# Decays at the chunk ends of an RWKV-7 layer: through DRAM rows in place of two TensorE transposes

## Chip, cores and metric

The kernel runs on one core of one Trainium2 chip. The metric is the device time of one execution in microseconds (us), as the median of several runs. Engines are called as in the profile: PE (TensorE, matrix products and transposes), DVE (VectorE), ACT (ScalarE), POOL (GpSimd) and SP (SyncE, whose queue issues nearly all DMAs here).

## The reference, cut to what matters

The model is a trunk of two layers over 256 tokens of width 1024. Each layer has a half-step SwiGLU FFN, a mixer, and another half-step FFN; the mixer of layer 0 is a short convolution, that of layer 1 is RWKV-7 time mixing with 16 heads of 64 channels. Only the recurrence of the time mixing is touched:

```python
w_log = -softplus(-(w0 + tanh(xw @ w1) @ w2)) - 0.5
decay = exp(-exp(w_log))                       # per token and channel
def step(S, inp):                              # S: one 64x64 state per head
    r_t, w_t, k_t, v_t, a_t, b_t = inp
    sa = einsum('bhij,bhj->bhi', S, a_t)
    S = S * w_t[:, :, None, :] + sa[..., None] * b_t[:, :, None, :] + v_t[..., None] * k_t[:, :, None, :]
    y = einsum('bhij,bhj->bhi', S, r_t)
    return S, y
```

Tokens are worked in chunks of 64. From one chunk to the next the state of each head is multiplied, channel by channel, by the product of the 64 decays of the chunk. These products are what the change fetches in another way.

## The kernel before, in words

Everything but the recurrence is dense products: FFN in layer 0, convolution, FFN, FFN of layer 1, the inputs of the time mixing, then the stage of the heads (some 700 to 885 us of the span), then the last FFN. Every fp32 product is made of three matmuls on a high and a low part (`product`, L110 to L114).

In the stage of the heads (`rwkv_heads`, L829) the work is cut into 8 units n: four groups q of four heads, each with two halves t of 128 tokens, and each unit holds two chunks of 64 tokens. Four generators give the steps of a unit:

- `front(n)` (L841): gates and decays of the unit. A product with a lower triangle (`cum`) sums the logs of the decays; ACT makes from it `P` (L874), the running product of the decays with tokens on the partitions, then `PP` (L875) and later `iP` (L883). POOL makes `rt` from `P` (L877), DVE finishes `PP` (L881); PE transposes `PP`, `rt`, `b`, `iP` (tile `wT`), and multiplies them into the matrices `G`. DVE masks these into `br` (L930) and `ar` (L933). Eight small DMAs copy `b` and `iP` from partition to partition into `bkt`. In its last step, PE transposes `P` (tile `PT`, two transposes of 128x128), and ACT copies from the result four columns, the chunk ends, into `pc` (L940 to L944).
- `wkv_inverse` (L490), run through `inverse(n)` (L949): the inverse of a triangular matrix by doubling, products `pair` on PE, `pb` on DVE, `xr` on ACT. At its steps 6 and 8 it issues the loads `hvu` for the unit's two chunks.
- `chain(n)` (L960, `wkv_chunk` L542): the recurrence over the chunks: `rc` on ACT (L558), products `ch` on PE, and at the end of a chunk DVE multiplies the new state by `pc` (L581).
- `finish(n)` (L967): norm and gate of the output.

Between these, `filler()` puts pieces of dense products into PE's stream (tile `pj`), whose weights come as loads `hl_n` of 512 KB from DRAM into 8 buffers, issued by `feed()` on SP.

The order of all of this is written by hand. `score` (L1069) is a list of strings in which F, I, C, N, `*` and L mean the next step of the front of the unit after next, of the next unit's inverse, of the chain, of the finish, a filler, and a feed. PE's and SP's instructions keep the order of the program (`mm`, `tp` and `load` ask for it, L48 to L57), and ACT's and DVE's do so inside `manual_schedule`. So every engine is a queue: an instruction that waits holds all behind it.

Two sizes matter for the change. `P` has one buffer: `T2` (L835) makes a tile with `bufs=1`, so the front of the next unit writes its `P` into the memory that the unit before has used. And the PSUM banks that `front` uses (`tr_bank`, L87) are two in turn: one front takes `z`, `cum`, `wT`, `wT`, `G0`, `G1` and `PT`, seven in all, each of which waits until the bank before the last is read out.

Further, SP's DMAs signal on eight semaphores in turn (they are called DMAHW0 to DMAHW7 in lists of waits), and a DMA is issued when the eighth before it has landed.

Of the kernel before, what the change touches and what calls it, by code (L numbers as in the profile page):

```python
# [10 lines left out]
F32 = mybir.dt.float32  # L11
# [14 lines left out]
class Trunk:  # L26
# [802 lines left out]
    def rwkv_heads(self, pool, prm, krv, lora, gT, g2, rows, row_tile, P, loaded, follow,  # L829
                   first_weights, first):  # L830
        nc = self.nc
# [4 lines left out]
        s4 = lambda name, b=2: pool.tile([128, 4], F32, name=name, bufs=b)  # L836
        us, o = [], {}
# [3 lines left out]
        def front(n):  # L841

            q, t = divmod(n, 2)
            ts, cs = slice(t * 128, t * 128 + 128), slice(q * 256, q * 256 + 256)
            u = dict(bon=s4("bon", 4), hvu=[])
            us.append(u)
            k, r = (krv[q, i][:, t] for i in "kr")
            P, PP, kk, am, rt = (T2(i) for i in ("P", "PP", "kk", "am", "rt"))
# [10 lines left out]
            s, a = sa[:, 0], sa[:, 1]  # L859
# [5 lines left out]
            cp = self.tr_bank("cum")  # L865
# [47 lines left out]
            f = lambda z: z.rearrange("p c q t -> p (c q) t")  # L913
# [11 lines left out]
            yield  # L925
            nc.vector.copy_predicated(x0, by4(self.strict).bitcast(mybir.dt.uint32), f(gb[:, :, :, 0]))
            u["inv"] = inverse(n)
            next(u["inv"])
            yield
# [7 lines left out]
                    self.load(bkt[ro, c, :, e], self.tokens(iP, c, e))  # L937
                yield

            cp = self.tr_bank("PT")[:, 0:256]  # L940
            for p in range(2):
                self.tp(cp[:, p * 128:p * 128 + 128], P[:, p * 128:p * 128 + 128])
            u["pc"] = s4("pc", 3).rearrange("p (q c) -> p q c", q=2)
            nc.scalar.copy(u["pc"], cp.rearrange("p (q c s) -> p q c s", q=2, c=2)[:, :, :, 63])  # L944
            nc.vector.tensor_reduce(u["bon"], hd(am), AX.X, ALU.add)
            nc.vector.tensor_scalar(u["bon"], u["bon"], 0.5, None, op0=ALU.mult)
            yield
# [1 line left out]
        def inverse(n):  # L949
            q, t = divmod(n, 2)  # L950
            for i, _ in enumerate(self.wkv_inverse(pool, us[n], n % 2, self.pair[:, :, 0:256])):
                if i in (6, 8):
                    c = i // 2 - 3
                    h = pool.tile([128, 2, 2, 64], F32, name="hvu", bufs=6)
                    for e in range(2):
                        self.load(h[64 - 64 * e:128 - 64 * e, :, e], self.tokens(krv[q, "v"][:, t], c, e))
                    us[n]["hvu"].append(h)
                yield
# [93 lines left out]
        def filler():  # L1052
# [27 lines left out]
            'CNCL*NCC*NL*CC*LNNCNC*LCC*NNL*CC*L',  # L1080
        )
        fronts = (step for n in range(8) for step in front(n))
        feed()
        for _ in score[0]:
# [118 lines left out]
```

## Time and profile before

| what | value |
|---|---|
| runs before | 1086.74, 1086.78, 1088.98 us; median 1086.78 |
| profiled execution | 1088.63 us, its span 1086.9 us |
| PE busy | 1060.1 us, 98% of the span |
| DVE, ACT, POOL busy | 686.5, 528.8, 100.1 us (63%, 49%, 9%) |
| DMA | 259.39 MB, 239 GB/s on average, q1 busy 72.3% of 16 engines |
| chain that ended last | PE 73%, issue 18%, DVE 5% |

The span runs from the first to the last instruction; some 1.7 us of the execution's time lie around it. The chain that ended last is followed back from the last instruction, at each step to what released it. "Issue" in it is time in which an engine waited for nothing that the profile shows. The table is an average over stages; what a change in the stage of the heads is worth must be read there.

### The profile page before, as it was taken

What the parts mean: (1) busy time and instruction counts of PE and PEld (TensorE: products, weight loads), DVE (VectorE), ACT (ScalarE), POOL (GpSimd) and SP (SyncE); (2) the same over time, 40 slices, a digit from 0 to 9 for tenths busy, and PEclk for the clock granted to TensorE, in tenths of its full rate; (3) what the DMA queues carried; (4) which work ended last, traced back from release to release, by engine and by line L of the source; (5) the groups of instructions that cost most, each with busy time, mean ns of one, the idle gap of its engine ahead of it and who ended that gap; (6) DMA issues with size and microseconds to landing.
All of it is one profiled execution on the core that took longest, in us unless ns stands there. A gap on an engine that the chain in (4) does not pass through costs nothing.

```text
span 1086.9 us, 16688 instructions
## 1 busy us (share of the span) xinstructions
PE 1060.1 (98%) x6480; PEld 872.9 (80%) x6480; DVE 686.5 (63%) x980; ACT 528.8 (49%) x781; POOL 100.1 (9%) x179
## 2 busy tenths in 40 slices
PE   7999999999999999999999999999998999999997
PEld 5888888788878888887888888998877668888885
DVE  5665554787667565466665544758998866555444
ACT  7555543655555554455555442344645426444342
POOL 7000000000130000000000001122423210000000
PEclk9999999999999999999999999999999999999999
DMA  9999867698779996778988871866555855656541
GB/s 287 298 292 289 297 224 247 210 360 271 236 266 339 302 307 233 246 242 280 332 295 271 320 271 51 312 233 192 170 145 148 252 172 183 187 184 213 184 164 39
DMA packets 178167, 259.39 MB, mean 239 GB/s; under 512 B 24238, under 2 KB 142758, under 8 KB 178088
## 3 DMA queue, kind: packets, MB, share of 16 engines
q1 hardware_dynamic: 178088, 258.32, 72.3%
q8 instruction: 51, 0.84, 0.3%
q14 instruction: 28, 0.23, 0.1%
HBM read 216.34 MB, written 38.80 MB: 235 GB/s over the span
## 4 chain that ended last, share of the span: by engine, by line
PE 73%; issue 18%; DVE 5%; ACT 1%; DMA 1%; SPq 1%; POOL 0%; POOLq 0%; DVEq 0%; ACTq 0%
PE gu L113 10%; PE gu L114 10%; PE gu L112 10%; PE acc L113 5%; PE acc L114 5%; PE acc L112 5%; PE pj L112 2%; PE pair L114 2%; PE pair L113 2%; PE pair L112 2%; PE ci L113 2%; PE ci L114 2%; PE ci L112 2%; PE pj L113 2%; PE pj L114 2%
## 5 line engine op out<-in xcount | busy, mean ns | idle before, releaser
L107 DVE TENSOR_TENSOR lo_gu<-raw_gu,hi_gu 128x2048 fp32r<-128x2048 f32 (+2 forms) x92 | 198.4, 2160 | 110.2 <-ACT hi_gu L106 108.0
L113 PE MATMUL gu<-lo_gu,xh 128*128 128x512 f32 x640 | 253.5, 396 | 2.8 <-DVE lo_gu L107 2.7
L114 PE MATMUL gu<-hi_gu,xl 128*128 128x512 f32 x640 | 253.3, 396 | 0.0
L112 PE MATMUL gu<-hi_gu,xh 128*128 128x512 f32 x640 | 251.1, 395 | 0.7 <-ACT xh L178 0.7
L106 ACT CAST hi_gu<-raw_gu 128x2048 fp32r<-128x2048 f32 (+2 forms) x92 | 164.9, 1796 | 34.9 <-DMA raw_gu<-in_ffn_w_gu_dram 12.0
L107 DVE TENSOR_TENSOR lo_o<-raw_o,hi_o 128x2048 fp32r<-128x2048 f32 x48 | 109.2, 2291 | 110.5 <-ACT hi_o L106 109.2
L113 PEld LDWEIGHTS gu<-lo_gu,xh 128*128 128x128 f32 x640 | 120.9, 189 | 28.0 <-DVE lo_gu L107 4.3
L106 ACT CAST hi_o<-raw_o 128x2048 fp32r<-128x2048 f32 x48 | 90.7, 1908 | 103.4 <-PE acc L114 61.5
L112 PEld LDWEIGHTS gu<-hi_gu,xh 128*128 128x128 f32 x640 | 120.9, 189 | 25.0 <-ACT xh L178 1.1
L114 PEld LDWEIGHTS gu<-hi_gu,xl 128*128 128x128 f32 x640 | 120.8, 189 | 23.6 <-DVE xl L180 0.4
L113 PE MATMUL acc<-lo_o,ah 128*128 128x512 f32 (+1 forms) x316 | 122.4, 387 | 1.4 <-DVE lo_o L107 1.4
L114 PE MATMUL acc<-hi_o,al 128*128 128x512 f32 (+1 forms) x316 | 122.5, 388 | 0.0
L112 PE MATMUL acc<-hi_o,ah 128*128 128x512 f32 (+1 forms) x316 | 117.5, 388 | 0.0
L150 POOL TENSOR_TENSOR rs<-ms,fixed 128x1 f32<-128x1 f32 x14 | 11.2, 798 | 819.7 <-DVE ms L148 819.5
L345 ACT ACTIVATE s<-gu,rs 128x256 f32<-128x256 f32 x80 | 38.0, 475 | 98.4 <-PE gu L114 98.3
L113 PEld LDWEIGHTS acc<-lo_o,ah 128*128 128x128 f32 x316 | 59.4, 188 | 13.6 <-DVE lo_o L107 1.8
L112 PEld LDWEIGHTS acc<-hi_o,ah 128*128 128x128 f32 x316 | 59.4, 188 | 11.9
L114 PEld LDWEIGHTS acc<-hi_o,al 128*128 128x128 f32 x316 | 59.4, 188 | 11.9
L117 ACT CAST ah<-aT 128x512 fp32r<-128x512 f32 x44 | 25.8, 585 | 82.5 <-PE aT L351 82.5
L349 DVE SCALAR_TENSOR_TENSOR a<-gu,rs,s 128x256 f32<-128x256 f32 x80 | 38.3, 480 | 36.4 <-ACT s L345 36.4
L601 ACT CAST hl_p<-hl_p 128x512 fp32r<-128x512 f32 x72 | 44.3, 624 | 29.5 <-DMA hl_p<-in_rwkv_w_rkv_dram 16.9
L602 DVE TENSOR_TENSOR hl_p<-hl_p 128x512 fp32r<-128x512 f32 x72 | 48.2, 686 | 8.0 <-ACT hl_p L601 8.0
(270 smaller groups left out, 1662.8 us busy)
## 6 DMA issues: line engine op xcount, KB each, us to landing
raw_gu<-in_ffn_w_gu_dram SPq DMA_DIRECT2D x164, 512.0 KB, 5.6
raw_o<-in_ffn_w_d_dram SPq DMA_DIRECT2D x44, 1024.0 KB, 5.9
parts<-hl_p SPq DMA_DIRECT2D x72, 512.0 KB, 7.0
hl_n<-parts SPq DMA_DIRECT2D x52, 512.0 KB, 4.7
hl_p<-in_rwkv_w_rkv_dram SPq DMA_DIRECT2D x48, 256.0 KB, 7.4
raw_ci<-in_conv_w_in_dram SPq DMA_DIRECT2D x14, 512.0 KB, 6.9
raw_ci<-in_conv_w_in_dram SPq DMA_DIRECT2D x4, 1024.0 KB, 10.0
raw_o<-in_conv_w_out_dram SPq DMA_DIRECT2D x4, 1024.0 KB, 8.7
```

Source lines behind the costliest of these rows:

```text
L106: nc.scalar.copy(hi[:, ks], raw[:, ks])
L107: nc.vector.tensor_tensor(lo[:, ks], raw[:, ks], hi[:, ks].bitcast(F32), ALU.subtract)
L112: keep(mm(out, xh, wh, start=start, stop=False))
L113: keep(mm(out, xh, wl, start=False, stop=False))
L114: keep(mm(out, xl, wh, start=False, stop=stop))
L117: keep(self.nc.scalar.copy(hi, src))
L150: self.last_rs = nc.gpsimd.tensor_tensor(rs, ms[:, 1:2], self.nhalf[:, 0:1], ALU.pow)
L345: act = nc.scalar.activation(s, ps[t][:, 0:256], AF.Silu, scale=rstd[t])
L349: nc.vector.scalar_tensor_tensor(a, ps[t][:, 256:512], rstd[t], s, ALU.mult, ALU.mult)
L601: nc.scalar.copy(hi, lo)
L602: nc.vector.tensor_tensor(lo.bitcast(F32R), lo, hi.bitcast(F32), ALU.subtract)
```

## The change

`P` is no longer transposed. At the end of the front, two DMAs of one row each (partitions 63 and 127 of `P`, 256 channels, 1 KB) store the two chunk ends into a new DRAM tile `ends`. At step 4 of the unit's inverse, two DMAs read these rows back, so that each partition gets its channels: 256 pieces of 4 bytes each. The consumer of `pc` (L581) stays.

```diff
-            cp = self.tr_bank("PT")[:, 0:256]
-            for p in range(2):
-                self.tp(cp[:, p * 128:p * 128 + 128], P[:, p * 128:p * 128 + 128])
-            u["pc"] = s4("pc", 3).rearrange("p (q c) -> p q c", q=2)
-            nc.scalar.copy(u["pc"], cp.rearrange("p (q c s) -> p q c s", q=2, c=2)[:, :, :, 63])
+            u["ends"] = self.dram.tile([2, 256], F32, name=f"ends{n}")
+            for c in range(2):
+                self.load(u["ends"][c:c + 1], P[64 * c + 63:64 * c + 64])
             nc.vector.tensor_reduce(u["bon"], hd(am), AX.X, ALU.add)
...
             for i, _ in enumerate(self.wkv_inverse(pool, us[n], n % 2, self.pair[:, :, 0:256])):
+                if i == 4:
+                    us[n]["pc"] = pc = s4("pc", 3).rearrange("p (c q) -> p q c", q=2)
+                    with nc.allow_non_contiguous_dma("a channel on each partition"):
+                        for c in range(2):
+                            self.load(pc[:, :, c], us[n]["ends"][c].rearrange("(q p) -> p q", p=128))
                 if i in (6, 8):
```

On PE the eight pairs of transposes go, and nothing else of the stage moves. At the end of front 0 (`z` is the first product of front 1):

```order
 L113 MATMUL pj<-hl_n,xvh 128x256
 L114 MATMUL pj<-hl_n,xvl 128x256
-L57 MATMUL PT<-fixed,P 128x128 x2
 L54 MATMUL z<-w_5291,wT 128x256
 L54 MATMUL z<-a_5293,aT 128x256
```

The two transposes are gone, and with them one turn of the two PSUM banks: `z` now takes the bank of `G0`, where it took that of `G1`.

On SP, at the end of front 1 (it follows the eight `bkt` DMAs of the unit; `parts` are the split weights in DRAM):

```order
 L50 DMA hl_n<-parts_2825 128x1024
 L50 DMA hl_n<-parts_2912 128x1024
+L50 DMA ends_6176<-P 1x256 x2
 L50 DMA hl_n<-parts_2914 128x1024
+L50 DMA pc<-ends_6176 128x2x1 x2
 L50 DMA hvu<-pv 64x2x64 x2
 L50 DMA hl_n<-parts_3001 128x1024
```

The stores stand behind two weight loads, and the loads of `pc` one weight load later, ahead of `hvu`. At the end of front 0 it is two weight loads, the stores, three weight loads, `pc`. In fronts 2 to 6 the stores come straight behind `bkt`; in front 7 they stand behind two weight loads and four loads for the last FFN, with `pc` straight behind them.

On ACT, in front 2, with what each instruction waits for (semaphores of engines, and of DMAs as DMAHW), before:

```order
-L508 COPY xr_6250<-pair 128x512 [waits DVE_49]
-L874 ACTIVATE P<-cum,fixed 128x256 [waits DVE_49]
-L875 ACTIVATE PP<-PP,fixed 128x256
-L558 COPY rc<-ch 128x128 [waits PE_49]
-L508 COPY xr_6291<-pair 128x512 [waits DVE_49,Activation_49]
```

And with the change:

```order
+L508 COPY xr_6249<-pair 128x512 [waits DVE_49]
+L874 ACTIVATE P<-cum,fixed 128x256 [waits DMAHW4_49,DMAHW3_49,DVE_49]
+L875 ACTIVATE PP<-PP,fixed 128x256
+L558 COPY rc<-ch 128x128 [waits PE_49]
+L508 COPY xr_6290<-pair 128x512 [waits DVE_49,Activation_49]
```

`P` of a front now also waits for two DMAs, the stores of the front before, which read its buffer. All fronts from 1 to 7 have this wait. `PP`, `rc` and the next `xr` stand behind it on ACT.

## Rows read from the trace of the kernel before

**Rows 1.** Busy time of the engines in two stretches (columns in the header).
```profile
core 0: us, PE busy (x) PEld busy (x) DVE busy (x) ACT busy (x) POOL busy (x), PEclk, DMA share, GB/s
720.00:760.00 40.00, 39.18 (x543) 33.66 (x543) 27.88 (x71) 18.94 (x50) 8.61 (x13) 1.00 0.68 217
...
800.00:840.00 40.00, 36.31 (x550) 29.29 (x548) 35.66 (x93) 20.75 (x59) 13.79 (x18) 1.00 0.56 150
```

**Rows 2.** Tile PT: duration ns min/median/max, first and last start.
```profile
L57 PE MATMUL PT<-fixed,P x16: 271/272/299, 721.3 to 856.0; 128*128 128x128 f32 x16
L944 ACT COPY pc<-PT x8: 162/162/168, 721.7 to 856.3; 128x4 f32<-128x4 f32 x8
```

**Rows 3.** PE timeline at some removed transposes: start us, us, and idle before.
```profile
755.07 0.41 PE L57 MATMUL PT<-fixed,P 128*128 128x128 f32 x2 [0.36 <-DVE br L930]
...
755.41 0.46 PE L54 MATMUL pair<-xr,p 64*64 64x64 f32 x16
...
794.22 0.31 PEld L574 LDWEIGHTS ch<-hvu,bkt 128*64 128x64 f32 x8 [0.16 <-ACT y L570]
...
832.90 0.41 PE L57 MATMUL PT<-fixed,P 128*128 128x128 f32 x2 [1.30 <-DVE br L930]
```

**Rows 4.** Waits of PE, 640 to 900 us: total us, times, longest.
```profile
PE PT L57 <- DVE br L930: 1.9, 3, 1.3
...
PE z L54 <- DVE ar L933: 0.6, 2, 0.4
```

**Rows 5.** SP's timeline: third weight load after front 0, and after front 1.
```profile
725.44 0.38 SPq L50 DMA_DIRECT2D hl_n<-parts  x1
...
744.25 0.38 SPq L50 DMA_DIRECT2D hl_n<-parts  x1
```

**Rows 6.** DMAs issued at 724.97, 729.55, 729.96 and 743.77 us: KB, us to landing.
```profile
hl_n<-parts SPq DMA_DIRECT2D x1, 512.0 KB, 4.2
...
hl_n<-parts SPq DMA_DIRECT2D x1, 512.0 KB, 6.4
...
hvu<-pv SPq DMA_DIRECT2D x1, 32.0 KB, 6.2
...
hl_n<-parts SPq DMA_DIRECT2D x1, 512.0 KB, 4.9
```

**Rows 7.** DMA issued at 723.63 us, behind no weight load: KB, us to landing.
```profile
bkt<-iP SPq DMA_DIRECT2D x1, 32.0 KB, 1.9
```

**Rows 8.** ACT timeline: P of fronts 1 and 2, and rc behind the latter.
```profile
727.08 0.47 ACT L874 ACTIVATE P<-cum,fixed 128x256 f32<-128x256 f32 x1 [0.27 <-DVE PP L873]
...
742.93 0.47 ACT L874 ACTIVATE P<-cum,fixed 128x256 f32<-128x256 f32 x1
...
743.70 0.25 ACT L558 COPY rc<-ch 128x128 f32<-128x128 f32 x1
```

**Rows 9.** DVE and PE timelines behind P of front 1.
```profile
727.98 0.66 DVE L881 SCALAR_TENSOR_TENSOR PP<-kk,PP 128x256 f32<-128x256 f32 x1 [0.21 <-ACT PP L875]
...
729.36 0.38 PE L57 MATMUL wT<-fixed,PP 128*128 128x128 f32 x2
```

**Rows 10.** PE timeline behind P and rc of front 2.
```profile
744.25 0.40 PE L54 MATMUL ch<-rc,tt 64*64 64x64 f32 x8
```

**Rows 11.** SP's hvu at the place of front 7's stores, and its landing.
```profile
860.21 0.62 SPq L50 DMA_DIRECT2D hvu<-pv  x1
...
hvu<-pv SPq DMA_DIRECT2D x1, 32.0 KB, 6.7
```

**Rows 12.** Last bkt of fronts 2 and 6 (SP), P of fronts 3 and 7 (ACT).
```profile
755.14 0.61 SPq L50 DMA_DIRECT2D bkt<-iP  x1
...
761.10 0.48 ACT L874 ACTIVATE P<-cum,fixed 128x256 f32<-128x256 f32 x1
...
830.19 0.61 SPq L50 DMA_DIRECT2D bkt<-iP  x1
...
839.50 0.48 ACT L874 ACTIVATE P<-cum,fixed 128x256 f32<-128x256 f32 x1
```

## Prediction

> **What bounds the kernel now.** I read four views: busy time by stretch, the tile and the waits of the removed work, the timelines of SP, ACT and PE around the new wait, and the landing times of single DMAs.
>
> In the stage of the heads PE is busy 39.2 of 40 us while fronts 1 to 3 run (720 to 760 us) and still 36.3 of 40 at 800 to 840, where DVE has 35.7 [rows 1]. The clock is granted in full in both stretches. So time taken from PE is worth nearly its whole length early in the stage and less later on; and since PE's queue is in order, a wait of PE in this stage is time lost to the end: what follows is dense products again, which no earlier engine can shorten.
>
> **What goes.** Sixteen transposes of 272 ns and eight ACT copies of 162 ns [rows 2]. ACT is half idle; its 1.3 us count nothing by themselves. For PE the pair takes less than twice 272 ns, since the two overlap: the product after it starts 0.34 us behind it (755.07 to 755.41) [rows 3]. Eight pairs: 2.7 us. With them go the waits of the PSUM turn: PT waited for `br` 1.9 us in three places, and `z` for `ar` 0.6 us in two [rows 4]; `z` will wait for `br`, which DVE makes earlier. The upper bound of the gain is thus 2.7 + 1.9 + 0.6 = 5.2 us, the lower bound nothing.
>
> I don't take the whole. Fronts 0 and 1 give nothing, because PE runs into the new wait right behind them (below). Front 2 gives 0.5 (the pair, and part of its 0.36 us wait). Fronts 3 and 5 give some 0.6 each with the wait of `z`. In front 4 the product two places on stood waiting for an ACT copy anyway (`y`, 0.16 us) [rows 3], so nothing comes through. In front 6 PT waited 1.30 us [rows 3], but the same copies stand behind it; I take 0.5. Front 7 gives 0.3. That is 2.5 us; as DVE is as busy as PE from front 4 on [rows 1], I take **2.0 us**.
>
> **What comes: a wait of ACT for a store.** `P` has one buffer. The next front's `P` could be written as soon as POOL and PE had read the old one; now it must wait until two rows have been stored to DRAM, and the store stands on SP behind whatever SP issues before it. So the price is: landing of the stores minus the time at which `P` wants to start, less the slack until PE needs what hangs on it.
>
> Front 0 to 1. The stores come where SP issues its third weight load, at 725.44 us [rows 5]. Ahead of them are two loads of 512 KB; the second, issued at 724.97, takes 4.2 us and lands at 729.2 [rows 6]. How does a small DMA behind a big one land? The row for it: a load issued at 729.55 takes 6.4 us (735.95), and `hvu`, 32 KB, issued 0.4 us behind it, takes 6.2 (736.16) [rows 6]: 0.2 us after the big one. A small DMA with nothing big ahead of it takes 1.9 [rows 7]. Between these ends I take the first, since two big loads do stand ahead: the stores land at 729.4. `P` of front 1 started at 727.08 [rows 8], so it is 2.3 us late. On it hang `PP`, DVE's product (done at 728.64) and PE's transposes of `PP` at 729.36 [rows 9]: slack 0.7. **PE stalls 1.6 us.**
>
> Front 1 to 2. The stores come at the place of the load issued at 744.25 [rows 5], behind one issued at 743.77 that takes 4.9 us: 748.7 [rows 6]. SP itself is late here, as the load of `pc` of unit 0 held it until 729.4 plus two issues, which I price at 0.6 each like `hvu` [rows 11]: 730.6, against the 729.55 of the load that followed. Of this 1.1 us some 0.5 go into SP's own waits before `bkt`; I take 0.6 late. The stores land at 748.7 + 0.6 + 0.2 = 749.5. `P` of front 2 started at 742.93 [rows 8], before SP had even come to the stores' place: it is 6.5 us late. Behind it on ACT stands `rc`, 0.77 us after, 0.25 long [rows 8], and PE needs `rc` at 744.25 [rows 10]: slack 0.3. So PE is 6.2 us late there, of which 1.6 are counted already: **4.6 us more**. The `pc` load of unit 1 holds SP until the same moment, and its loads behind come about as late as PE, so no second price is set on them.
>
> Fronts 2 to 6 cost nothing. There the stores follow `bkt` at once: 755.14 + 0.61, two issues of 0.6 and 1.9 make 758.9, and `P` wants 761.10 [rows 7, 12]; in front 6, 830.80 + 1.2 + 1.9 = 833.9 against 839.50 [rows 12]. Their `pc` loads find SP idle or the stores landed. If SP were 2 us later than PE in front 2, this cover would be gone, at 1 us for 1 us.
>
> Front 7. No `P` follows, but the loads of `pc` stand right behind the stores, and these behind loads for the last FFN. DMAs issued there took 6.7 us (`hvu` at 860.21) [rows 11], so SP stands until about 867 before it issues `hvu` for the last unit. By then the DMA queues are empty, and the landing is the short one. I take 0.2 us, with 1.5 as the upper bound.
>
> **Sum.** 1.6 + 4.6 − 2.0 + 0.2 = +4.4 us. Against the profiled execution's 1088.63 us that is 1093.0; that execution was 1.85 above the median of 1086.78, so in terms of the median the forecast is **1091.2 us**. With the gain between 5.2 and 0.5 and the tail between 0 and 1.5, this case alone gives 1087.8 to 1094.0, mostly 1089 to 1094.
>
> **Rivals.**
> *A: the stores overtake the loads.* They are one row of 1 KB each. With the 1.9 us of [rows 7], the first pair lands at 725.44 + 0.6 + 1.9 = 727.9: `P` 0.9 late, 0.2 at PE. The second lands at 744.25 + 0.6 + 1.9 = 746.8, `P` 3.9 late, PE 3.6 late in all. Minus 2.0 and plus 0.2: +1.8, or 1088.6. For it: so small a store may not have to share with the loads' many pieces. Against it: `hvu` didn't overtake.
> The Trainium skill, page "DMA: Bandwidth & Descriptors", section "Anatomy of one DMA", gives for GpSimd's DMAs a fixed cost of about 2.0 us plus bytes over 436 GB/s, and names nothing that stands ahead; for 1 KB that is an estimate of 2.0 us, and the time would be A's. The trace agrees for a DMA that stands alone (1.9) [rows 7] and not for one behind a big load (6.2) [rows 6].
>
> *B: not slower.* The freed PE time counts in full, as each pair stands in PE's stream where PE is nearly full [rows 1], and the stores overtake. Gain 5.2 against 3.6: −1.6, so 1085.2. It decides at `P` of front 2: PE is late by the landing minus 743.2, so with a gain of 5.2 the store must land before 748.4. Against it are the places where the next product waits for ACT anyway [rows 3].
>
> *C: the stores land later still.* They write to DRAM while 1 MB of loads is under way, and the two `pc` loads add 512 pieces of 4 bytes per unit to queues that are backed up at 730. No row has such pieces. With 6.2 us of landing (`hvu`'s) [rows 6] for both stores, the first pair lands at 732.2: `P` 5.1 late, PE 4.4. SP is then 3 us later, the second pair is issued near 748 and lands near 754.2: `P` 11.3 late, PE 11. Minus 2.0: +9, or 1095.8.
>
> *D: the tail.* SP's stand in front 7 makes `hvu` late for the last chunk: 1.3 more than the forecast, 1092.5. It lies inside the range.
>
> That the change doesn't do what it says is not likely: `P`'s new wait stands in ACT's list of instructions for fronts 1 to 7.
>
> **How the numbers follow.** Chances: the forecast (with D) 0.68, A 0.14, B 0.05, C 0.13. The range goes from a little under A to most of the way to C: 1088.0 to 1095.0. A measurement of this kernel can tell about 0.2%, 2.2 us, from no change, so "same" is 1084.6 to 1089.0: it holds nearly all of A and the lowest end of the forecast, 0.17. Faster, below that, is B's further end with a still larger gain: 0.04. Slower: 0.79.
>
> **What would show it.** Right: ACT's `P` of front 2 stands idle some 6 us waiting for a DMA `ends<-P`, PE's `ch<-rc` behind it has an idle time of about 4 to 5 us, and PE's `wT<-PP` of front 1 one of 1 to 2 us; fronts 3 to 7 show no such wait; the landing of `ends` is 4 to 5 us in fronts 0 and 1 and about 2 in fronts 2 to 6. PE's busy time falls by some 4 us and its idle time grows by more. Wrong: `P` of front 2 starting within 4 us of its front's `xr` (A or B), or further waits of PE in fronts 3 to 7, on `hl_n` or `hvu`, which would mean that SP stays late.

## The result, and the profile of the changed kernel

The change is slower. The changed kernel ran in 1092.37 to 1097.99 us, median of five 1094.09; beside it the kernel before had a median of 1088.39 us. The ratio of all these runs is 1.0062, interval 1.0048 to 1.0076: +6.7 us (the two medians alone are 5.7 us apart; the ratio is what is used below). A second measurement of the same kernel (r_after, below) gave 1.0071 [1.0059, 1.0083], +7.7 us. I had forecast +4.4 us: the direction held, the size did not.

The profiled execution took 1092.37 us (span 1090.6). It is the fastest of the five. The profiled execution of the kernel before had lost 1.5 us to the clock in its first 20 us, which this one did not; so where the two are compared below, each time is taken from the first product of the stage, `z` of front 0.

The two stretches of [rows 1], after:

```profile
720.00:760.00 40.00, 34.62 (x478) 29.67 (x477) 23.77 (x59) 16.80 (x44) 8.28 (x12) 0.96 0.62 191
800.00:840.00 40.00, 36.74 (x559) 29.71 (x561) 35.85 (x95) 21.05 (x58) 13.77 (x18) 1.00 0.53 154
```

Between 720 and 760 us PE lost 4.6 us of work (39.18 before), and the clock is 0.96 in place of 1.00. The later stretch hardly differs. ACT's timeline, for `P` of fronts 1, 2 and 3 ([rows 8] before):

```profile
727.61 0.47 ACT L874 ACTIVATE P<-cum,fixed 128x256 f32<-128x256 f32 x1 [2.53 <-DMA ends<-P]
746.64 0.47 ACT L874 ACTIVATE P<-cum,fixed 128x256 f32<-128x256 f32 x1 [3.86 <-DMA ends<-P]
765.30 0.48 ACT L874 ACTIVATE P<-cum,fixed 128x256 f32<-128x256 f32 x1
```

`P` waits for the stores in fronts 1 and 2, and in no later one. What PE makes of it, in its timeline ([rows 9, 10] before):

```profile
729.32 0.41 PE L57 MATMUL wT<-fixed,PP 128*128 128x128 f32 x2 [1.52 <-DVE PP L881]
...
747.72 0.45 PE L54 MATMUL ch<-rc,tt 64*64 64x64 f32 x8 [3.50 <-ACT rc L558]
...
748.83 0.41 PE L112 MATMUL pj<-hl_n,xrh 128*128 128x256 f32 x1
749.04 0.41 PE L113 MATMUL pj<-hl_n,xrh 128*128 128x256 f32 x1
...
750.75 0.63 PE L57 MATMUL wT<-fixed,PP 128*128 128x128 f32 x2
```

PE stands for 1.52 us and then for 3.50 us. Behind the second stand the products start every 0.21 us, where they started every 0.12 before, and the pair of transposes of `PP` takes 0.63 us where it took 0.38. The pair, and one of the stretches below, in the kernel before:

```profile
746.11 0.38 PE L57 MATMUL wT<-fixed,PP 128*128 128x128 f32 x2
```

```profile
748.00:750.00 2.00, 1.93 (x29) 1.61 (x26) 1.94 (x6) 1.72 (x5) 1.53 (x2) 1.00 1.06 350
```

The stretches of the changed kernel show why (same columns as [rows 1]):

```profile
744.00:746.00 2.00, 0.22 (x8) 0.00 (x0) 0.00 (x0) 0.00 (x0) 0.00 (x0) 1.00 1.05 384
746.00:748.00 2.00, 0.28 (x8) 0.29 (x8) 0.46 (x1) 1.02 (x3) 0.72 (x1) 1.00 0.76 261
748.00:750.00 2.00, 2.00 (x15) 1.93 (x12) 1.51 (x4) 0.99 (x3) 1.07 (x3) 0.55 0.29 33
750.00:752.00 2.00, 2.00 (x21) 1.70 (x24) 0.85 (x2) 0.94 (x4) 0.18 (x1) 0.60 0.66 199
```

The granted clock falls to 0.55 and 0.60: for most of these 4 us TensorE ran at the lower of its two levels, 1.2 GHz. From `ch<-rc` to `wT<-PP` it took 3.03 us, before 1.86 (744.25 to 746.11): the fall cost 1.17 us, which no step of the forecast holds.

SP's queue, at the stores of fronts 0, 1 and 7 and at the last norm's rows ([rows 5, 11] before; the last line is of the kernel before):

```profile
723.95 0.53 SPq L50 DMA_DIRECT2D ends<-P  x2
...
727.35 1.05 SPq L50 DMA_DIRECT2D pc<-ends  x2
...
742.84 0.54 SPq L50 DMA_DIRECT2D ends<-P  x2
...
746.38 0.90 SPq L50 DMA_DIRECT2D pc<-ends  x2
...
862.48 0.62 SPq L50 DMA_DIRECT2D ends<-P  x2
867.31 0.90 SPq L50 DMA_DIRECT2D pc<-ends  x2
...
876.73 0.33 SPq L50 DMA_DIRECT2D rows<-in_rwkv_ln_w_dram  x1
```

```profile
869.86 0.38 SPq L50 DMA_DIRECT2D rows<-in_rwkv_ln_w_dram  x1
```

The trace holds no landing of a store, but what waits for one bounds it: SP goes on to `pc` 3.4 us after the first store of front 0 (723.95 to 727.35) and 3.5 us after that of front 1 (742.84 to 746.38), and ACT's `P` starts 3.7 and 3.8 us after it. So the first stores take neither the 4 to 5 us of the forecast nor the 1.9 of a DMA that stands alone. The weight load right ahead of the stores of front 0, issued at 723.48 (KB, us to landing, as in [rows 6]):

```profile
hl_n<-parts SPq DMA_DIRECT2D x1, 512.0 KB, 4.2
```

It landed at 727.70, just after SP had gone on to `pc` (727.35) and `P` had started (727.61). For the load ahead of the stores of front 1 the trace has no landing. In front 7 SP stands from 863.1 to 867.3 before `pc`. All its loads behind come later, among them the rows `ln_w` and `ln_b` for the norm of units 6 and 7. DVE and PE then wait (the last line is PE's of the kernel before, without idle time ahead):

```profile
882.85 0.43 DVE L993 TENSOR_TENSOR y<-y,rows 128x256 f32<-128x256 f32 x1 [1.16 <-DMA rows<-in_rwkv_ln_w_dram]
...
884.98 0.44 PE L57 MATMUL oT<-fixed,y 128*128 128x128 f32 x2 [0.77 <-DVE y L996]
```

```profile
881.29 0.38 PE L57 MATMUL oT<-fixed,y 128*128 128x128 f32 x2
```

The waits of PE from 640 to 900 us ([rows 4]; total us, times, longest) name the three places; `PT` and its waits are gone, and those of `z` for `ar` too:

```profile
PE ch L54 <- ACT rc L558: 3.9, 2, 3.5
PE wT L57 <- DVE PP L881: 2.5, 2, 1.5
...
PE oT L57 <- DVE y L996: 0.8, 1, 0.8
```

**The account.** How late an instruction is against the kernel before, in us from `z` of front 0 (the instruction's start less its start before, less the same difference for that `z`), for most kernels that the next section speaks of:

| kernel | `z`, front 2 (739) | `ch<-rc` (744) | `wT<-PP` (746) | `z`, front 7 (835) | `ch<-rc` (867) | `ch<-rc` (880) | last `oT` (892) |
|---|---|---|---|---|---|---|---|
| changed | +1.31 | +4.99 | +6.16 | +4.42 | +4.29 | +4.29 | +5.27 |
| r_after | +1.48 | +5.50 | +6.67 | +4.91 | +4.80 | +4.78 | +6.97 |
| e4_no_pc | −0.40 | −0.40 | −0.39 | −2.03 | −2.24 | −0.79 | −0.84 |
| e1_two_p | +0.47 | +0.46 | +0.46 | −0.78 | −1.01 | +0.46 | +0.81 |
| e2_early | −0.43 | +0.09 | +0.15 | −1.24 | −1.36 | +0.05 | +0.06 |
| e9_two_names | −0.42 | +0.46 | +0.51 | −0.90 | +0.48 | +1.95 | +1.96 |
| e6_front2 | −0.40 | +5.51 | +6.99 | +5.97 | +5.82 | +7.27 | +8.19 |
| e7b_fill | +2.11 | +6.25 | +6.30 | +4.75 | +4.61 | +6.05 | +6.86 |
| e8_late_pc | −0.40 | +4.15 | +5.64 | +4.63 | +4.43 | +5.90 | +5.91 |
| e3_both | +0.86 | +2.18 | +2.23 | +2.38 | +2.36 | +3.81 | +4.94 |
| x12_both | 0.00 | +0.17 | +0.22 | +0.37 | +0.37 | +0.38 | +4.11 |
| x13_rows | 0.00 | 0.00 | +0.01 | +0.47 | +0.45 | +1.17 | +7.40 |
| x14_nowait | +0.02 | +0.02 | +0.03 | −0.01 | −0.03 | −0.03 | −0.04 |
| e11_merged | −0.40 | −0.38 | −0.33 | −1.78 | −2.01 | −2.02 | −2.02 |
| x15_best (the same kernel) | −0.40 | −0.28 | −0.22 | −1.64 | −1.88 | −0.44 | −0.42 |

The changed kernel, step by step: −0.22 by the end of front 0, +1.53 in front 1, +3.68 up to `ch<-rc` of front 2, +1.17 by the clock, −1.87 by freed PE time up to 867, +0.98 at the tail: +5.27. The second measurement's profile gives −0.22, +1.70, +4.02, +1.17, −1.87 and +2.17: +6.97.

### The profile page after: what moved, and what is told of

It reads as the page before. It is cut to its first block, busy times and chain, and to the rows that moved or that the text cites. A ratio compares the mean times of both kernels' runs of the same rounds, so it can differ in the third digit from the quotient of the medians.

```text
span 1090.6 us, 16698 instructions
## 1 busy us (share of the span) xinstructions
PE 1058.8 (97%) x6464; PEld 871.1 (80%) x6464; DVE 686.1 (63%) x980; ACT 528.3 (48%) x773; POOL 97.4 (9%) x179
## 4 chain that ended last, share of the span: by engine, by line
PE 72%; issue 18%; DVE 4%; ACT 2%; DMA 2%; SPq 1%; POOL 0%; POOLq 0%; ACTq 0%; DVEq 0%
PE gu L113 10%; PE gu L114 10%; PE gu L112 9%; PE acc L113 5%; PE acc L114 5%; PE acc L112 5%; PE pair L114 2%; PE pair L112 2%; PE pair L113 2%; PE pj L112 2%; PE ci L113 2%; PE ci L114 2%; PE ci L112 2%; PE pj L113 2%; PE pj L114 2%
```

## Experiments

All ratios are to the kernel before on the same chip, with a 95% interval in brackets. Theory W is the forecast's: the loss is ACT's wait for `P`'s buffer. Theory K is added: PE's standing brings the clock down. Q is the rival that SP's queue itself is what costs. Each profile is one execution; where it and the ratio differ, the ratio stands for the time and the profile for the place.

### The wait taken away: e1_two_p, e2_early, e9_two_names

e1_two_p:

```diff
-            P, PP, kk, am, rt = (T2(i) for i in ("P", "PP", "kk", "am", "rt"))
+            PP, kk, am, rt = (T2(i) for i in ("PP", "kk", "am", "rt"))
+            P = T2("P", 2)
```

> The change with two buffers for P, nothing else. Theory W (the loss is ACT's wait for the buffer of P, and what PE's standing costs): no wait of ACT on `ends<-P` is left, PE has no idle above 0.5 us at `wT<-PP` of front 1 or `ch<-rc` of front 2, the granted clock is 1.00 from 740 to 760 us. From the profiles, the offset to the kernel before, measured from the start of the stage (5.3 us in the changed kernel), falls to -1.9 (freed PE time) + 1.0 (tail) = -0.9 us: a ratio to the kernel before of 0.998 to 1.000. Rival Q (SP's queue is what costs: the small DMAs and the 4-byte pieces hold it up, and P's wait only shows it): most of the loss stays, ratio 1.003 to 1.006.

Measured: 0.9996 [0.9987, 1.0006]. No wait of `P` for `ends`, PE busy 19.18 of the 20 us from 740 to 760 as before, clock 1.00 there. W holds for the loss of 6.7 us, which is gone with one more buffer; what the removed work is worth (below) does not come through. The profile shows something new in front 0, though:

```profile
706.88 1.28 ACT L875 ACT_TABLE_LOAD   x1 [1.77 <-DVE PP L874]
708.18 0.47 ACT L875 ACTIVATE P<-cum,fixed 128x256 f32<-128x256 f32 x1
```

`P` of front 0 now waits for two semaphores, and the wait for DVE stands at the table load ahead of it, which before had run while DVE worked. PE was 0.84 us later at the first `wT`.

e2_early (one buffer, the same four DMAs, only the place of the stores changes):

```diff
+            u["ends"] = self.dram.tile([2, 256], F32, name=f"ends{n}")
+            for c in range(2):
+                self.load(u["ends"][c:c + 1], P[64 * c + 63:64 * c + 64])
             for e, re, ro in own:
                 nc.vector.tensor_tensor(ar[ro, :, :, e].rearrange("p c q s t -> p (c q) (s t)"),
...
-            u["ends"] = self.dram.tile([2, 256], F32, name=f"ends{n}")
-            for c in range(2):
-                self.load(u["ends"][c:c + 1], P[64 * c + 63:64 * c + 64])
```

> The change with the two stores issued ahead of the eight `bkt` DMAs and not behind them and the weight loads; P keeps one buffer. Theory W: the stores land some 5 us earlier than in the changed kernel (727.6 and 746.6 there, against 727.1 and 742.9 at which P wants to start), so P waits 0 to 0.3 us; and in front 7 the stores are ahead of the loads of the last FFN, so SP no longer stands before `pc`, and the 0.8 us of the tail go too: -1.9 + 0.2 = -1.7 us, ratio 0.997 to 0.9995. Rival Q: as many small DMAs as in the change, so the loss stays, ratio 1.003 to 1.006. A third case: the stores now stand in front of `bkt` on SP and make `bkt` 0.5 us later, and PE waits for it: ratio 0.999 to 1.001.

Measured: 0.9991 [0.9981, 1.0002]; `P` waits for no DMA in any front, and the tail's wait is gone. So the place of the stores behind the weight loads was the cause of the loss, not the way through DRAM as such; but of the 2.7 us that the removed work is worth (below), only 1.0 comes through.

e9_two_names: `P = T2("P" if n % 2 == 0 else "Pb")`, two buffers without the table load's wait.

> The change with a second buffer for P, by a second name that odd units use; in e1_two_p the second buffer made the load of ACT's table for front 0 wait for DVE, which cost 0.84 us and is absent here. Theory: of the 2.7 us that the removed work is worth, 0.4 us go to SP's lateness in the fronts and 0.3 to 1.0 at the tail: ratio 0.9982 to 0.9990. Rival (SP's turn of eight DMAs is what costs: the small DMAs push the loads of k_a and r_k back): ratio 0.9995 to 1.001, and DVE's `am` of front 2 waits more than 1 us for a DMA `rows<-in_rwkv_k_a_dram`.

Measured: 0.9997 [0.9989, 1.0006], so my figure missed and the rival's was right: in the profile DVE's `am` of front 2 waits 1.9 us for the rows `k_a`, and PE is 0.88 us later there. Something beside `P`'s wait takes back what the removed work is worth. The rival's reason, the turn of eight, is another matter: x14_nowait below, with as many DMAs, speaks against it.

### What the removed work is worth: e4_no_pc

The transposes, the copy and their bank go; `pc` is a tile of zeros, so this kernel leaves out what carries the state from chunk to chunk.

```diff
-            cp = self.tr_bank("PT")[:, 0:256]
...
-            nc.scalar.copy(u["pc"], cp.rearrange("p (q c s) -> p q c s", q=2, c=2)[:, :, :, 63])
+            u["pc"] = self.zero4.rearrange("p (q c) -> p q c", q=2)
```

> The kernel before without the transposes, the copy and their PSUM bank; `pc` is a tile of zeros, so the state is not carried from chunk to chunk by the decays. It is the worth of the removed work alone. Theory W: -1.9 us by the offsets of the changed kernel (front 2 to the end of front 7), -2.0 by the forecast, plus up to 0.5 for fronts 0 and 1: ratio 0.9975 to 0.9985. Rival: the removed PE time counts in full, with its waits 5.2 us, ratio 0.995. Other rival: the stage waits for DVE and the chain anyway, ratio 0.9995 to 1.0005.

Measured: 0.9975 [0.9966, 0.9983], −2.7 us. In its profile 2.24 us are gained by 867 us, in steps of 0.2 to 0.6 per front (none in front 4), and then 1.45 lost again to a fall of the clock at 868 to 872 (below).

### The price of the small DMAs: e3_both, x12_both, x13_rows, x14_nowait

Transposes as before, the DMAs beside them with a result that nobody reads, two buffers for `P`: e3_both with `T2("P", 2)`, x12_both with the two names.

```diff
+            cp = self.tr_bank("PT")[:, 0:256]
...
+            nc.scalar.copy(u["pc"], cp.rearrange("p (q c s) -> p q c s", q=2, c=2)[:, :, :, 63])
             u["ends"] = self.dram.tile([2, 256], F32, name=f"ends{n}")
...
-                    us[n]["pc"] = pc = s4("pc", 3).rearrange("p (c q) -> p q c", q=2)
+                    pc = s4("pc2", 3).rearrange("p (c q) -> p q c", q=2)
```

> The transposes stay and deliver `pc`; the four small DMAs per unit are issued as in the change, their result is not read; P has two buffers. It is the price of the DMAs alone. Theory W: SP's queue and the pieces cost nothing in fronts 0 to 6, and 0.8 to 1.0 us at the tail, where SP stands before the load of `pc`: +1.0 us, ratio 1.000 to 1.002. Rival Q: the price of the DMAs is the loss itself, +4 to +6 us, ratio 1.004 to 1.006.

> As e3_both (the transposes stay and deliver `pc`, the four DMAs per unit are issued beside them and not read), with the second buffer of P by a second name, so without the late table load of that run. It is the bare price of the four DMAs and the measure for the next two runs. From e3_both (+2.6) and from e9_two_names less the run without the work (+2.4): ratio 1.0018 to 1.0028. Rival: the table load was the price there, ratio 1.0010 to 1.0017.

Measured: e3_both 1.0024 [1.0013, 1.0034], x12_both 1.0027 [1.0016, 1.0037]. The DMAs alone cost 2.6 to 2.9 us, as much as the removed work is worth; theory W's figure for e3_both (+1.0) was too small and Q's (+4 to +6) too large. The place differs: in e3_both's profile 1.3 us of it go in front 2, where DVE's `am` waits 2.5 us for the rows `k_a`, and 1.1 at the tail. x12_both is level with the kernel before up to 880 us (+0.38) and loses at the tail. SP's queue, DVE, PE and the stretches there:

```profile
857.13 0.56 SPq L50 DMA_DIRECT2D ends<-Pb  x2
862.21 1.04 SPq L50 DMA_DIRECT2D pc<-ends  x2
```

```profile
879.24 0.42 DVE L999 TENSOR_TENSOR y<-y,rows 128x256 f32<-128x256 f32 x1 [2.09 <-DMA rows<-in_rwkv_ln_w_dram]
```

```profile
881.62 0.44 PE L57 MATMUL oT<-fixed,y 128*128 128x128 f32 x2 [1.96 <-DVE y L1002]
```

```profile
880.00:882.00 2.00, 0.38 (x3) 0.38 (x4) 1.28 (x4) 0.21 (x2) 0.58 (x1) 1.00 0.00 0
882.00:884.00 2.00, 2.00 (x14) 1.37 (x13) 1.36 (x4) 0.85 (x4) 0.00 (x0) 0.74 0.00 0
884.00:886.00 2.00, 2.00 (x6) 1.52 (x6) 1.44 (x3) 0.07 (x1) 0.00 (x0) 0.50 0.00 0
886.00:888.00 2.00, 2.00 (x10) 1.60 (x9) 1.02 (x2) 0.64 (x2) 0.00 (x0) 0.91 0.00 0
```

SP stands 4.5 us before `pc`, the norm's rows are late, PE stands 1.96 us, and the clock falls behind it for another 1.6 us (+2.50 at `oT` of 881, +4.07 at the next transposes). Which property of the DMAs does it? x13_rows reads `ends` in 64 pieces of 16 bytes; x14_nowait keeps the 4-byte pieces but reads a row that nothing writes:

```diff
-                            self.load(pc[:, :, c], us[n]["ends"][c].rearrange("(q p) -> p q", p=128))
+                            self.load(pc[64 * c:64 * c + 64], us[n]["ends"][c].rearrange("(p f) -> p f", f=4))
```

```diff
-                            self.load(pc[:, :, c], us[n]["ends"][c].rearrange("(q p) -> p q", p=128))
+                            self.load(pc[:, :, c], prm["ln_w"][c * 256:c * 256 + 256].rearrange("(q p) -> p q", p=128))
```

> As x12_both, but the two loads bring the rows in 64 pieces of 16 bytes each, in place of 256 of 4 bytes; they wait for the stores as before. Theory S (the price is SP's: its turn of eight DMAs and its stand until the stores have landed): the same as x12_both within 0.0006. Rival P (the 4-byte pieces hold up the DMA queues): a half or more of the price goes, ratio 0.0010 or more below x12_both.

> As x12_both, with the same 4-byte pieces, but the two loads read a constant row in DRAM that nothing writes, so SP doesn't stand until the stores have landed. Theory S1 (SP's stand at `pc`): most of the price goes, ratio 1.0000 to 1.0010, and the rows for the last norm are no longer late at the tail. Theory S2 (the turn of eight: four more DMAs between the weight loads): more than half of it stays, ratio 1.0012 to 1.0025. Rival P: nothing goes.

Measured: x13_rows 1.0041 [1.0025, 1.0057], x14_nowait 1.0000 [0.9991, 1.0010]. x13_rows is 1.5 us slower than x12_both and not level with it, as I had said; the intervals overlap, and in its profile SP stands 5.4 us at the tail. The pieces are not the price, nor is the number of DMAs; **SP's stand at `pc` is all of it**, to within the 1 us of x14_nowait's interval. x14_nowait's SP goes on at once:

```profile
857.84 1.07 SPq L50 DMA_DIRECT2D ends<-Pb  x2
858.95 1.19 SPq L50 DMA_DIRECT2D pc<-in_rwkv_ln_w_dram  x2
```

and its profile lies within 0.05 us of the kernel before at every place of the table.

### The clock: r_after, e6_front2, e7_fill, e7b_fill

r_after is the changed kernel again.

> The changed kernel as it is, a second time, beside the three below. In its first profile PE stood for 3.5 us before `ch<-rc` of front 2 and the granted clock was then 0.55 and 0.60 from 748 to 752 us, which cost 1.2 us. Theory K (the fall follows from PE's standing): the clock is again below 0.7 in some stretch of 2 us within the 6 us behind the stand, ratio to the kernel before 1.004 to 1.007. Rival: the fall was chance, and the clock stays at 1.00 there.

Measured: 1.0071 [1.0059, 1.0083]. PE stands 3.85 us before `ch<-rc`, then the clock is 0.72 and 0.50 from 748 to 752: K's sign came again. The ratio lies just above the range.

e6_front2: `P = T2("P" if n else "Pa")`, so that only front 2 waits.

> The change, with a buffer of its own for P of front 0: P of front 1 waits for no store, P of front 2 still waits for that of front 1 (and so on). Theory W: PE has no idle at `wT<-PP` of front 1 and one of 3.5 to 5 us before `ch<-rc` of front 2 (the landing of the store is set by SP, which is partly set by PE), then the clock's fall of 1.2 us. Of the 6.2 us that the changed kernel is late at `wT<-PP` of front 2 (from the start of the stage, against the kernel before), 4.5 to 6.2 are left; ratio 1.003 to 1.006. Rival: the two stands are independent and add up, so that 1.5 us go: ratio 0.0014 below that of the changed kernel.

Measured: 1.0062 [1.0049, 1.0075]. One stand of 5.74 us in place of 1.5 and 3.5, and a longer fall of the clock, which begins within the stand:

```profile
746.00:748.00 2.00, 0.23 (x4) 0.23 (x6) 0.41 (x1) 1.02 (x3) 0.72 (x1) 0.72 0.85 314
748.00:750.00 2.00, 2.00 (x15) 1.88 (x14) 1.56 (x4) 0.95 (x3) 1.06 (x3) 0.50 0.29 34
750.00:752.00 2.00, 2.00 (x11) 1.77 (x9) 0.85 (x2) 0.79 (x3) 0.13 (x1) 0.50 0.42 125
752.00:754.00 2.00, 2.00 (x31) 1.46 (x32) 0.67 (x2) 1.63 (x5) 1.32 (x2) 0.57 0.52 170
```

The two stands do not add up: what PE gains in front 1 it waits for in front 2. Counted from `z` of front 0, `P` of front 2 starts after 43.03 us here, 43.02 in r_after and 42.51 in the changed kernel's first profile: the moment does not come earlier when PE does. More is left at `wT<-PP` (6.99) than my 4.5 to 6.2. The ratios do not tell the two theories apart (1.0062 here, 1.0071 in r_after, with intervals that overlap); the profiles do. This is how the forecast counted them ("of which 1.6 are counted already").

e7_fill put 20 transposes of the identity ahead of `ch<-rc`, into its own bank; e7b_fill 22 into the bank `fin`:

```diff
+        if first and self.fill:
+            d = self.bank("fin", "g")
+            for _ in range(22):
+                self.tp(d[:, 0:128], self.ident)
+            self.fill = False
         for p, e, re, ro in both:
             self.mm(ps[re, 1, p], tt[re, c, p], rc[re, p])
```

> The change, with 20 transposes of the constant identity put on PE ahead of `ch<-rc` of front 2, into a part of the bank that the product behind them overwrites; nothing waits for them, and they fill most of PE's stand. Theory K (the clock falls because PE stood): the granted clock stays at 1.00 from 746 to 754 us, and between `ch<-rc` and `wT<-PP` of front 2 no more than 0.1 us is lost against the kernel before, in place of 1.2: ratio some 0.001 below that of the changed kernel. Rival (it falls for another reason, the DMA traffic or by chance): as many us are lost there as in the changed kernel.

> As the run e7_fill, but the 22 transposes of the constant identity go to the PSUM bank of the finish, which nothing uses at this point, so that they wait for nothing and PE works through its stand before `ch<-rc` of front 2 (in e7_fill they stood behind `rc` themselves). Theory K (the clock falls because PE stood): no idle of PE over 0.6 us from 740 to 750 us, the granted clock at 1.00 in every stretch of 2 us from 744 to 756, no more than 0.2 us lost between `ch<-rc` and `wT<-PP` of front 2 against the kernel before; ratio 1.0045 to 1.0062, against 1.0071 of the changed kernel in its second measurement. Rival (it falls for another reason): stretches below 0.7 as in the changed kernel, ratio 1.0065 to 1.008.

e7_fill tells nothing of K by its design: the transposes, in the bank that ACT reads `rc` from, waited for `rc` themselves (PE stood 5.5 us; ratio 1.0094 [1.0075, 1.0113]). In e7b_fill they ran (PE's timeline, and stretches):

```profile
744.55 2.62 PE L57 MATMUL g<-fixed 128*128 128x128 f32 x22
748.59 0.45 PE L54 MATMUL ch<-rc,tt 64*64 64x64 f32 x8 [1.42 <-ACT rc L558]
```

```profile
746.00:748.00 2.00, 1.17 (x11) 0.93 (x9) 0.00 (x0) 0.49 (x2) 0.00 (x0) 1.00 0.97 357
748.00:750.00 2.00, 1.41 (x16) 1.34 (x17) 1.55 (x3) 1.02 (x3) 1.51 (x3) 1.00 0.40 81
750.00:752.00 2.00, 2.00 (x34) 1.60 (x32) 0.76 (x3) 1.60 (x7) 0.29 (x2) 1.00 0.58 162
```

PE still stood 1.42 us, more than the 0.6 I had expected, but not 3.5. With PE at work the clock stays at 1.00, and between `ch<-rc` and `wT<-PP` 0.05 us is lost in place of 1.17. So this fall follows from PE's standing, in one profile. The ratio, 1.0082 [1.0063, 1.0100], missed my figure: in the profile `P` waited 7.7 us in two places, not 6.4, for landings that differ between executions. So the runs do not show the 1.1 us, the profile does. In front 1 PE stood 2.32 us in this profile and the clock stayed at 1.00; in e7_fill it stood 2.40 us there and the clock fell.

### Later loads, fewer DMAs, another queue: e8_late_pc, e11_merged, x15_best, e10_pool

e8_late_pc has the stores of e2_early, and `pc` loaded at step 8 behind `hvu`.

> The stores ahead of `bkt`, as in the run above, and the loads of `pc` behind the loads `hvu` of step 8, so that SP comes to them when the stores have long landed. Theory: SP no longer stands at `pc`, the loads of k_a and r_k for front 2 come in time, and of the worth of the removed work (2.7 us in the run without it) 2.0 to 2.7 are left: ratio 0.9975 to 0.9985. Rival: the issues themselves (0.6 us per pair) or the 4-byte pieces cost, as in the run with the stores ahead of `bkt` alone: ratio 0.999 to 1.000. A third case: `pc` now lands too late for the first state product (L581): DVE waits there for a DMA `pc<-ends`, ratio above 1.

Measured: 0.9996 [0.9984, 1.0007]. Neither the forecast nor the third case; the runs spread from 1084.12 to 1092.72 us, and the profiled one is the slowest of the twelve. In it SP has issued `pc` by 735.7 us and the loads of `k_k` and `k_a` for front 2, right behind, only at 738.27 and 738.98 (before: 733.19 and 734.29). This is another stand than that at `pc`. What SP waited for between 735 and 740 us (total us, times, longest):

```profile
SPq L50 <- DMA hl_n<-parts: 3.6, 2, 2.5
```

The load that it stood for longest was issued at 727.54, the eighth DMA before `k_k`: SP's turn of eight. In x14_nowait, with as many DMAs at other places, that turn cost nothing that the runs show. DVE's timeline:

```profile
742.71 0.64 DVE L862 SCALAR_TENSOR_TENSOR am<-sa,rows 128x256 f32<-128x256 f32 x1 [5.55 <-DMA rows<-in_rwkv_k_a_dram]
```

PE stood 3.75 us behind it, and the clock fell to 0.50. So in this execution a late `pc` only moved the crowding of SP's queue to the next urgent load. What a usual execution loses, the one profile does not show.

e11_merged: two names for `P`, the store ahead of `bkt`, one store and one load per unit:

```diff
+            self.load(u["ends"], P[63:128:64])
...
+                        self.load(pc.rearrange("p q c -> p c q"), us[n]["ends"].rearrange("c (q p) -> p c q", p=128))
```

> Two buffers for P as in the run above, the store ahead of `bkt`, and one DMA in place of two both for the store (2 rows) and for the load of `pc` (512 pieces of 4 bytes): two DMAs per unit where the change has four. Theory (what is left of the price is SP's turn of eight and its stands at `pc`): half the DMAs, half the price, and no tail: -2.7 + 0.3 = -2.4 us, ratio 0.9973 to 0.9985, faster than any version so far. Rival (the 4-byte pieces themselves hold up the queues): no better than e2_early, ratio 0.999 to 1.000.

> e11_merged as it is, a second time: the best version so far. Ratio 0.9978 to 0.9992, as in its first measurement (0.9985).

Measured: 0.9985 [0.9976, 0.9993], and a second time 0.9989 [0.9980, 0.9998]: faster than the kernel before by 1.2 to 1.6 us, and than the change by 8 to 9. Its first profile keeps 2.02 us of the gain to the end, with the clock at 1.00 throughout the stage; the second profile (x15_best) keeps 1.88 up to 867 us and 0.42 to the end, as the clock falls in between. That the merging and not the second buffer brings the difference to e2_early (0.9991) isn't shown; the intervals overlap.

e10_pool: as e11_merged, with both DMAs on POOL's queue.

> As e11_merged, but both DMAs are issued by POOL, so that SP's queue is that of the kernel before. Theory: SP's lateness is gone altogether, and POOL, busy 9% of the span, has room: ratio 0.9970 to 0.9980, close to the run without the work (0.9975). Rival: POOL stands at `pc` until the store has landed, or its issues take over 1 us each, and `rt` (front) and `am` behind them on POOL come late: PE waits at `wT<-PP` or `wT<-b`, ratio 0.999 to 1.003.

Measured: 0.9986 [0.9974, 0.9997], no better than e11_merged and short of my 0.9970 to 0.9980: POOL's issues take 0.6 to 0.9 us, and DVE still waited 2.9 us for `k_a` in the profile.

## Why the forecast held in direction and missed in size

- **The wait for the buffer: right.** It is in fronts 1 and 2 alone, as forecast, and a second buffer or an earlier store takes it away.
- **Front 1: right.** Forecast 1.6 us at PE, measured 1.53 and 1.70. `P` started 3.7 us after SP's issue of the first store.
- **Front 2: too large.** Forecast 4.6, measured 3.68 and 4.02. I took SP as 0.6 us late, and the store as landing 0.2 us behind the big load; SP was on time (742.84, against 744.25 for the load at this place before, in an execution that ran 1.5 us ahead), and `P` started 3.8 us after the issue. That lies between rival A's 1.9 and the 4.9 that the load ahead took in the kernel before. Whether the store overtook the load ahead of it here is not shown; the stores of front 0 landed a little before theirs, not 0.2 us behind.
- **Freed PE time: right.** Forecast −2.0, measured −1.87 in the change, with −0.22 in front 0 besides, and −2.24 to −2.7 alone. Front 4 gave nothing, as forecast.
- **The clock: missing.** No term for it; measured +1.17 in both profiles. The kernel before did show such a fall, where I had not looked: PE stood in part between 12 and 14 us, and the granted clock was then 0.65 and 0.50 (last section). That row would have told of a possible fall and not of a sure one: the changed kernel's PE was as little busy there (0.62 and 1.36 of 2 us), and its clock stayed at 1.00. In the stretches of [rows 1], where the clock was 1.00, PE had stood no more than 1.3 us at a time.
- **The tail: the step that failed most.** "I take 0.2 us, with 1.5 as the upper bound": measured +0.98 and +2.17. Alone, the four DMAs cost 2.6 to 2.9 us by the runs (e3_both, x12_both), in x12_both's profile nearly all of it here, the clock's fall included. SP's stand was forecast to within a us (863.1 to 867.3), but I looked only at `hvu` as its victim. The rows of the last norm stand further back in the same queue, and they are what PE waited for; rival D had the place and the wrong load.
- **The signs.** PE's waits behind `P` stood where they were forecast, at `wT<-PP` of front 1 and `ch<-rc` of front 2, and in no later front. But ACT stood idle before `P` of front 2 for 3.9 us and not some 6, and PE's busy time fell by 1.3 us (1060.1 to 1058.8) and not by some 4.

So the sum of 4.4 should have been 5.3 to 7.0, and the runs say 6.7 to 7.7. The median, 1094.09 us, lies in the range that I had set (1088.0 to 1095.0), but the room at its upper end was there for rival C, stores that land later still, and they landed earlier: that the range holds the time is luck. In runs alone: removed work −2.7, SP's stands +2.6 to +2.9, and `P`'s wait with its clock some +7 to +8 (both measurements of the changed kernel, 1.0062 and 1.0071, less 0.9997 of e9_two_names). The third is a difference and checks nothing; the first two make −0.1 to +0.2, and e9_two_names, which has just these, measured −0.3.

What stays open: why x13_rows is slower than x12_both; how much of `P`'s wait differs from one execution to the next, since profiles show single ones; why the runs lose 0.7 to 1.4 us more than the profiles' sums; and why the rows `k_k` (128 KB) land 5.3 us after their issue in the kernel before and 7.5 in e10_pool.

## What to carry to other kernels

A DMA that reads what an earlier DMA wrote is a wait of its queue, and everything behind it comes later: follow that queue to its end and price each load there, not the next one alone. A buffer that a store reads is held until the store has landed; store before the big loads, or give the buffer a twin. Where a change makes PE stand for as long as it did here (3.1 us and more), add a term for the clock behind it, read from a place in a trace where that has happened; for shorter stands, set it as a chance.

## What was not expected of the hardware

The granted clock fell to its lower level behind stands of PE in the middle of a dense stage. In the 18 profiles, from 700 to 895 us, it fell with each of the six stands of 3.1 us or more, behind two of four of 2.0 to 2.4, and behind the one of some 1.6 us that every kernel here has near 870 us in 11 of 18; three other stands of 1.4 to 1.7 us had none behind them. Each of the falls near 870 that the table can show cost 1.4 to 1.5 us (the columns 867 and 880). Once, in e9_two_names at 832 to 838 us, it fell with no stand above 0.51 us ahead, where PE had been busy 1.06 of 2 us. One kernel can thus differ by that much from one execution to the next: e11_merged and x15_best are the same kernel, 0.1 us apart up to 867 us and 1.6 us apart behind the fall. The profiled execution of the kernel before in its first us:

```profile
12.00:14.00 2.00, 0.70 (x4) 0.22 (x2) 0.72 (x4) 2.00 (x7) 1.61 (x8) 1.00 1.08 367
14.00:16.00 2.00, 1.38 (x6) 1.28 (x7) 2.00 (x6) 2.00 (x6) 1.85 (x3) 0.65 1.10 351
16.00:18.00 2.00, 2.00 (x6) 1.62 (x5) 2.00 (x5) 1.67 (x6) 1.85 (x4) 0.50 1.09 348
```

And 256 pieces of 4 bytes per load, which I had feared in rival C, cost nothing that can be measured (x14_nowait, 1.0000).
